# Two-layer hybrid decoder on one core: mixer operands without the norm's row factor, gates and branch products token-major

## The chip, the cores and the metric

The kernel runs on one core of a Trainium2 chip. Its time is the device time of one execution in microseconds (us), as the median of several runs. The engines are TensorE (PE, matmuls; PEld is its weight load), VectorE (DVE), ScalarE (ACT), GpSimd (POOL) and SyncE (SP, which issues most transfers). PE's results go to PSUM, which the kernel uses as eight banks; one bank holds a 128x512 tile of 32-bit numbers.

## What is computed

DEPTH = 2 layers over SEQ = 256 tokens with D_MODEL = 1024, all in 32-bit numbers:

```python
for l in range(DEPTH):
    h = rmsnorm(x, norm_mix[l])
    x = x + mixer_block(h, ...)
    x = x + cross_attention(rmsnorm(x, norm_xattn[l]), rmsnorm(mem, norm_mem[l]), ...)
    x = x + squared_relu_mlp(rmsnorm(x, norm_mlp[l]), w_up[l], w_down[l])
return rmsnorm(x, norm_final)

def rmsnorm(x, g):
    return x * rsqrt(mean(x * x, axis=-1, keepdims=True) + eps) * g

def mixer_block(h, ...):
    zin = h @ w_in
    (cq, ckv, kpe, sg_uv, gq, gk, gv, g_lr, g_og, dq, dk, dv, da, db, dz, gates) = split(zin)
    branches = stack([mla(...), spatial_gating(...), gla(...), deltanet(...)])  # 4 x (256, 256)
    proj = einsum('bsnw,nwd->bsnd', branches, w_branch)
    gate = sigmoid(gates).reshape(b, s, 4, 1024)
    return sum(gate * proj, axis=2) @ w_out
```

The factor `rsqrt(...)` of the norm is one number for each token (the row factor); `g` is one number for each of the 1024 features (the gain). A product of the normalised input can be taken without the row factor, and each row of the result multiplied by it.

## The kernel before

**Products.** A 32-bit operand is split into a high and a low part, and each product is three matmuls: high by high, low by high, high by low (`mm3`, L185 to L187). Weights arrive in order as a stream of blocks of 128x1024 (`half`): SP transfers two blocks at a time into one of three buffers, ACT casts the high part `wh` (L178), DVE subtracts for the low part `wl` (L181); four buffers each for `wh` and `wl` let this run ahead of PE. A buffer is written again only when PE has read it for the last time.

Two forms of product run on the stream. `gemm` keeps the weights as the stationary operand and moves 256 tokens past them, so its matmuls are 256 wide (N=256) and the result has features on the partitions. `gemm_tok` keeps 128 tokens as the stationary operand and moves 512 weight columns past them (N=512); its result is token-major: tokens on the partitions, one bank for each of two token halves t.

**Banks and pieces.** Three banks (tag "g") serve the streamed products, five (tag "s") all else. A bank is free when its eviction, an ACT or DVE instruction, has read it. Tiles of 128x512 in on-chip memory come from `new()`, a list of 44 pieces in which the piece freed first is given out first; `rel()` frees them. A new tile in a piece waits for the last reader of the old one.

**Order.** A scheduler decides before the run in what order each engine issues its instructions; on the chip each engine keeps that order, and waits on semaphores for the others. The gate products are independent of the mixers, so the order strews them between the mixers' small matmuls.

**A layer.** First `gemm` on `Norm.h`/`Norm.l`, which hold the input times the gain without the row factor; `ev_dn` multiplies by the row factor `rrow` when it evicts. Meanwhile the row factor is computed. Then `hn` = input × gain × row factor (L484, DVE), its high part `hh` (L487, ACT) and low part `hl` (L488, DVE). On these run `zin_rest` (four more column blocks and the token-major block `zs`), and the gates (L1077 evicts them through tanh, since sigmoid(z) = (tanh(z/2) + 1)/2). The mixers run beside the gates: among them the delta net (`dn_out`: L694 `u0`, L698, L703, L710, L724, where `uu` is evicted at L695 and L711) and the gated linear attention (`gla`: L789 makes the running sum `cum`, from it DVE makes the tiles `dd`, L814 to L821, ACT exponentiates them at L823, DVE multiplies them into `qt`, L856). `head_out` ends a branch; it makes a row factor `rb` (L774, ACT), turned by PE at L778.

Behind the mixers come the products on the memory (`mh`, `ml`; `mr` are its transfers, which ACT issues at L1110, `kx` the result), then `merge`: the four branch products of 128 features at a time, multiplied by the gates (L1092, DVE), added by POOL (L1093 and L1097), split into `mgh` and `mgl` (L1099, L1100), the operands of `w_out`. Cross attention and the MLP follow. The end of the program is a token-major product, whose eviction adds (L1239), squares (L1240, ACT), multiplies by the final gain `gf` (L1241, DVE) and scales (L1245, L1247).

Of the kernel before, what the change touches and what calls it, by code (L numbers as in the profile page):

```python
# [55 lines left out]
def decoder(ctx: ExitStack, tc: tile.TileContext, ws, xn_d, xt_d, mem_d, pos_d, fin_d, par_d, cst_d, msk_d, out_d):  # L56
# [59 lines left out]
    hh, hl = [], []  # L116
# [194 lines left out]
    class Norm:  # L311
        pass
# [33 lines left out]
    def gate_tile(i, dt=F32, name="gt"):  # L346
        return ap.tile([P, 2, T], dt, tag=f"gt{i}", name=nm(name))

    def operands(j, g, mix=False, parts=(slice(0, 2),), share=False):
        if mix and parts[0].start == 0:  # L350
            if j == 0:
                Norm.h, Norm.l = [], []
            Norm.h.append(gate_tile(2 * j, F32R, "xh")), Norm.l.append(gate_tile(2 * j + 1, F32R, "xl"))
        if True:
            dh, dl = (Norm.h[j], Norm.l[j]) if mix else (hh[j], hl[j])
            for p in parts:
                split_scaled(xs[j][:, p], g[:, 2 * j + p.start : 2 * j + p.stop], dh[:, p], dl[:, p], share)
# [67 lines left out]
    def layer(l):  # L425
# [50 lines left out]


        if l == 0:
            for d, n in ((hh, "hh"), (hl, "hl")):
                d.extend(ap.tile([P, 2, T], F32R, tag=f"{n}{j}", name=nm(n)) for j in range(4))  # L480
        for j in range(4):
            t = new(name="hn")
            for c in range(2):
# [4 lines left out]
            V.tensor_tensor(hl[j], t, hh[j].bitcast(F32), op=ALU.subtract)  # L488
# [594 lines left out]
        def merge(m):  # L1083
            wh, wl = half()
            for a in range(2):
                ps = pg.tile([P, 2, T], F32, tag="g", name=nm("g"))
# [5 lines left out]
                V.scalar_tensor_tensor(gt[m][a], gt[m][a], 1.0, ps, op0=ALU.add, op1=ALU.mult)  # L1092
            G.tensor_tensor(gt[m][0], gt[m][0], gt[m][1], op=ALU.add)  # L1093
# [344 lines left out]
```

## Time and profile before

| | |
|---|---|
| median of 3 runs | 1111.3 us (1110.27 to 1112.75) |
| profiled execution, its own time | 1111.81 us |
| its span in the trace | 1110.0 us |
| mean granted PE clock | 0.993 |
| PE busy | 1089.8 us, 8494 matmuls |
| DVE, ACT, POOL busy | 808.9, 586.8, 194.5 us |

The page of the profile lists the busy time of each engine, the chain that ended last (followed back from the last instruction to what released each step), and the costliest groups of instructions: line, engine, operation, tile written and tiles read, shapes, count, then busy time, mean duration in ns, and the idle time just before them with what ended it. Matmuls overlap, so a matmul's displayed duration is longer than the distance to the next one; the distance between starts is what PE spends. Rows of the timeline hold start, duration, engine, line, operation and tiles. The granted clock is the share of full speed that PE was given in a window.

### The profile page before, as it was taken

Reading aid. Unit: us, or ns where it says so; the run is one execution under the profiler, and the core shown is the slowest. Engines: PE = TensorE matmul, PEld = TensorE weight load, DVE = VectorE, ACT = ScalarE, POOL = GpSimd, SP = SyncE. Lnnn points to the kernel's source line nnn. Section 1 sums busy time; section 2 is a strip of 40 time slices with the busy share of each in tenths; the row PEclk is TensorE's granted clock in tenths of the full one; section 3 lists DMA queues with packets and bytes.
Section 4 is the critical chain, followed back from the end, with each engine's and each line's share of the span. In section 5 each row is a group of like instructions: output and inputs, shape, how many; then the busy total and the mean of one; then the engine's idle time right before and its main releaser. Section 6 shows DMA issues by size and latency. Waiting matters only on the chain.

```text
span 1110.0 us, 20715 instructions
## 1 busy us (share of the span) xinstructions
PE 1089.8 (98%) x8494; PEld 1046.4 (94%) x8494; DVE 808.9 (73%) x1411; ACT 586.8 (53%) x883; POOL 194.5 (18%) x176
## 2 busy tenths in 40 slices
PE   8899999999999999999999999999999999999996
PEld 8799999999998999999999899999999899998885
DVE  6999848779865866655679997686796777665454
ACT  6475564654644655544455646554454555555342
POOL 6223006108200200000102420310451011010000
PEclk9899999999999999999999999999999999999998
DMA  9344523454543455545545444244455334554541
GB/s 353 141 156 150 182 84 126 141 191 164 187 151 145 175 185 181 185 189 190 190 181 190 153 152 152 84 171 155 165 188 190 133 136 188 190 209 157 190 185 38
DMA packets 28319, 185.13 MB, mean 167 GB/s; under 512 B 3392, under 2 KB 3648, under 8 KB 6976
## 3 DMA queue, kind: packets, MB, share of 16 engines
q1 hardware_dynamic: 26208, 179.09, 44.3%
q10 hardware_dynamic: 2016, 4.72, 1.3%
q8 instruction: 66, 1.08, 0.4%
q14 instruction: 29, 0.24, 0.1%
HBM read 182.75 MB, written 1.05 MB: 166 GB/s over the span
## 4 chain that ended last, share of the span: by engine, by line
PE 94%; DVE 2%; DMA 1%; ACT 1%; issue 0%; ACTq 0%
PE g L186 28%; PE g L185 28%; PE g L187 28%; PE ps L185 1%; PE ps L186 1%; PE ps L187 1%; DMA mr<-memt 1%; PE ps L662 1%; PE ps L658 1%; PE ps L587 1%; DVE wl L181 1%; ACT wh L178 1%; DMA wr<-ws 0%; PE ps L575 0%; PE ps L967 0%
## 5 line engine op out<-in xcount | busy, mean ns | idle before, releaser
L181 DVE TENSOR_TENSOR wl<-wr,wh 128x1024 fp32r<-128x1024 f32 (+1 forms) x337 | 414.6, 1233 | 202.7 <-ACT wh L178 201.8
L178 ACT ACTIVATE wh<-wr 128x1024 fp32r<-128x1024 f32 (+1 forms) x337 | 355.0, 1057 | 352.1 <-PE g L186 254.4
L186 PE MATMUL g<-hl,wh 128*128 128x256 f32 x1280 | 362.5, 283 | 5.3 <-DVE hl L488 5.3
L187 PE MATMUL g<-hh,wl 128*128 128x256 f32 x1280 | 364.1, 285 | 0.0
L185 PE MATMUL g<-hh,wh 128*128 128x256 f32 x1280 | 362.8, 284 | 0.0
L186 PEld LDWEIGHTS g<-hl,wh 128*128 128x128 f32 x1280 | 242.3, 189 | 5.9 <-DVE hl L488 5.5
L187 PEld LDWEIGHTS g<-hh,wl 128*128 128x128 f32 x1280 | 242.0, 189 | 1.0 <-issue 0.3
L185 PEld LDWEIGHTS g<-hh,wh 128*128 128x128 f32 x1280 | 241.8, 189 | 0.7
L187 PE MATMUL g<-ah,wl 128*128 128x256 f32 x256 | 72.0, 281 | 0.0
L186 PE MATMUL g<-al,wh 128*128 128x256 f32 x256 | 71.9, 281 | 0.0
L185 PE MATMUL g<-ah,wh 128*128 128x256 f32 x256 | 71.8, 281 | 0.0
L325 POOL TENSOR_TENSOR sq<-sq,sq 128x512 f32<-128x512 f32 x14 | 21.1, 1506 | 244.8 <-ACT sq L317 244.6
L1093 POOL TENSOR_TENSOR gt<-gt,gt 128x512 f32<-128x512 f32 x16 | 35.6, 2227 | 92.8 <-DVE gt L1092 91.9
L186 PE MATMUL g<-wl,ah 128*128 128x512 f32 x128 | 50.2, 395 | 0.0
L187 PE MATMUL g<-wh,al 128*128 128x512 f32 x128 | 50.1, 394 | 0.0
L185 PE MATMUL g<-wh,ah 128*128 128x512 f32 x128 | 50.0, 395 | 0.0
L185 PEld LDWEIGHTS g<-ah,wh 128*128 128x128 f32 x256 | 48.2, 188 | 0.0
L187 PEld LDWEIGHTS g<-ah,wl 128*128 128x128 f32 x256 | 48.2, 188 | 0.0
L186 PEld LDWEIGHTS g<-al,wh 128*128 128x128 f32 x256 | 48.2, 188 | 0.0
L185 PE MATMUL g<-xh,wh 128*128 128x256 f32 x144 | 39.8, 282 | 1.5 <-ACT xh L298 1.5
L186 PE MATMUL g<-xl,wh 128*128 128x256 f32 x144 | 40.8, 285 | 0.3 <-DVE xl L307 0.3
L187 PE MATMUL g<-xh,wl 128*128 128x256 f32 x144 | 40.4, 283 | 0.0
(500 smaller groups left out, 2276.2 us busy)
## 6 DMA issues: line engine op xcount, KB each, us to landing
wr<-ws SPq DMA_DIRECT2D x166, 1024.0 KB, 4.8
wr<-ws ACTq DMA_DIRECT2D x4, 512.0 KB, 7.7
mr<-memt ACTq DMA_DIRECT2D x8, 256.0 KB, 4.0
par<-par SPq DMA_DIRECT2D x2, 778.0 KB, 6.9
x<-xt SPq DMA_DIRECT2D x3, 256.0 KB, 7.7
cst<-cst SPq DMA_DIRECT2D x1, 588.0 KB, 8.4
gf<-fin SPq DMA_DIRECT2D x2, 256.0 KB, 5.2
yt<-y ACTq DMA_DIRECT2D x2, 256.0 KB, 2.5
```

The lines of the kernel that those rows point to most:

```text
L178: i = S.activation(wh[:, p], r[:, p], AF.Copy)
L181: V.tensor_tensor(wl[:, p], r[:, p], wh[:, p].bitcast(F32), op=ALU.subtract)
L185: PE.matmul(out, ah, bh, start=start, stop=False)
L186: PE.matmul(out, ah, bl, start=False, stop=False)
L187: PE.matmul(out, al, bh, start=False, stop=stop)
L325: G.tensor_tensor(acc, acc, sq, op=ALU.add)
L587: PE.matmul(kk[o][:, 2 * i + c], kT[r, c, ts], src[r, c, ts], start=True, stop=True)
L658: PE.matmul(xp[:, h], M[:, h], Tm[:, h], start=True, stop=True)
L662: PE.matmul(up[:, h], X[t][:, h], U[:, h], start=True, stop=True)
L1093: G.tensor_tensor(gt[m][0], gt[m][0], gt[m][1], op=ALU.add)
```

## The change

The block that made `hn`, `hh` and `hl` for the mixer is removed. `zin_rest`, `zs` and the gates run on `Norm.h`/`Norm.l` (now X and XL) and the row factor enters where a result is evicted: as a row (`rrow`, DVE) for feature-major results, as a scale for each partition (`R.rs`, ACT) for token-major ones, halved (`R.rsh`) for the tanh. The gates become `gemm_tok`: 384 matmuls of N=512 in a layer instead of 768 of N=256. So do the branch products: 96 instead of 192. The merged product is then token-major; 16 PE transposes in a layer turn it, 8 for each half nb of the features, and ACT and DVE split it out of PSUM as 128x512. The additions run on POOL for n = 1 and 2 and on DVE for n = 3. The gate tiles of nb = 0 lie in the buffers of `hh`/`hl` (tags hx), those of nb = 1 in pieces. The host puts the weights in the new order. At the end of the program the last product with `gf` goes to a tile of its own.

```diff
     def operands(j, g, mix=False, parts=(slice(0, 2),), share=False):
...
+        dh, dl = (Norm.h, Norm.l) if mix else (hh, hl)
+        if parts[0].start == 0:
+            for i, d in enumerate((dh, dl)):
+                tag = f"xm{2 * j + i}" if mix else f"hx{2 * j + i}"
+                d[j] = ap.tile([P, 2, T], F32R, tag=tag, name=nm("xm" if mix else "hx"))
...
         def ev_dn(p, parts):
             if p == 0:
-                R.rrow = row_of(stat("rsmix"), name="rrow")
+                R.rs = stat("rsmix")
+                R.rrow = row_of(R.rs, name="rrow")
+                R.rsh = small(2, "rsh")
+                V.tensor_scalar(R.rsh, R.rs, 0.5, None, op0=ALU.mult)
...
-        for j in range(4):
-            t = new(name="hn")
-            for c in range(2):
-                V.scalar_tensor_tensor(
-                    t[:, c], xs[j][:, c], gain(4 * l)[:, 2 * j + c : 2 * j + c + 1], R.rrow, op0=ALU.mult, op1=ALU.mult
-                )
-            S.copy(hh[j], t)
-            V.tensor_tensor(hl[j], t, hh[j].bitcast(F32), op=ALU.subtract)
-            rel(t)
...
             def ev_rest(p, parts):
...
-                S.copy(t, ps)
+                V.tensor_tensor(t, ps, bc2(R.rrow), op=ALU.mult)
...
-            gemm(H, L, 8, 4, ev_rest)
+            gemm(X, XL, 8, 4, ev_rest)
...
-                S.copy(z, ps)
+                S.activation(z, ps, AF.Copy, scale=R.rs[:, t : t + 1])
...
-            gemm_tok(H, L, 8, ev_tok)
+            gemm_tok(X, XL, 8, ev_tok)
...
-        gt = [[None, None] for _ in range(8)]
-
-        def gates(m):
-            def evac(a, parts):
-                ps = parts[0][1]
-                if m < 4:
-                    t = gate_tile(2 * m + a)
+        gt = {}
+
+        def gates(nb, n):
+            def evac(t, ps):
+                if nb == 0:
+                    g = ap.tile([P, 512], F32, tag=f"hx{2 * n + t}", name=nm("gt"))
                 else:
-                    t = new(name="gt")
-                S.activation(t, ps, AF.Tanh, scale=0.5)
-                gt[m][a] = t
-            gemm(H, L, 8, 2, evac)
+                    g = new(shape=(P, 512), name="gt")
+                S.activation(g, ps, AF.Tanh, scale=R.rsh[:, t : t + 1])
+                gt[nb, n, t] = g
+
+            gemm_tok(X, XL, 8, evac)
 
         mgh, mgl = [], []
 
-        def merge(m):
-            wh, wl = half()
-            for a in range(2):
-                ps = pg.tile([P, 2, T], F32, tag="g", name=nm("g"))
-                for b in range(2):
-                    n = 2 * a + b
+        def merge(nb):
+            for n in range(4):
+                wh, wl = half()
+                for t in range(2):
+                    ps = pg.tile([P, 512], F32, tag="g", name=nm("g"))
+                    s = slice(128 * t, 128 * t + 128)
                     for k in range(2):
-                        c = slice(128 * (2 * n + k), 128 * (2 * n + k) + 128)
-                        mm3(ps[:, b], wh[:, c], wl[:, c], brh[n][:, k], brl[n][:, k], k == 0, k == 1)
-                V.scalar_tensor_tensor(gt[m][a], gt[m][a], 1.0, ps, op0=ALU.add, op1=ALU.mult)
-            G.tensor_tensor(gt[m][0], gt[m][0], gt[m][1], op=ALU.add)
-            if m % 2 == 0:
-                mgh.append(new(F32R, name="mgh")), mgl.append(new(F32R, name="mgl"))
-            t = gt[m][1][:, 0]
-            G.tensor_tensor(t, gt[m][0][:, 0], gt[m][0][:, 1], op=ALU.add)
-            dh, dl = mgh[-1][:, m % 2], mgl[-1][:, m % 2]
-            S.activation(dh, t, AF.Copy, scale=0.5)
-            V.scalar_tensor_tensor(dl, t, 0.5, dh.bitcast(F32), op0=ALU.mult, op1=ALU.subtract)
-            if m >= 4:
-                rel(gt[m])
-
-        for m in range(8):
-            gates(m)
+                        c = slice(512 * k, 512 * k + 512)
+                        mm3(ps, brh[n][:, k, s], brl[n][:, k, s], wh[:, c], wl[:, c], k == 0, k == 1)
+                    g, acc = gt[nb, n, t], gt[nb, 0, t]
+                    V.scalar_tensor_tensor(g, g, 1.0, ps, op0=ALU.add, op1=ALU.mult)
+                    if n:
+                        (V if n == 3 else G).tensor_tensor(acc, acc, g, op=ALU.add)
+            for j in range(2):
+                ps = bank()
+                for c in range(2):
+                    for t in range(2):
+                        o = 256 * j + 128 * c
+                        PE.transpose(ps[:, c, 128 * t : 128 * t + 128], gt[nb, 0, t][:, o : o + 128], ident)
+                a, b = new(F32R, name="mgh"), new(F32R, name="mgl")
+                S.activation(a, ps, AF.Copy, scale=0.5)
+                V.scalar_tensor_tensor(b, ps, 0.5, a.bitcast(F32), op0=ALU.mult, op1=ALU.subtract)
+                mgh.append(a), mgl.append(b)
+            if nb:
+                rel([gt[1, n, t] for n in range(4) for t in range(2)])
+
+        for nb in range(2):
+            for n in range(4):
+                gates(nb, n)
...
-        for m in range(8):
-            merge(m)
+        for nb in range(2):
+            merge(nb)
...
-                V.tensor_tensor(z, z, gf[nb], op=ALU.mult)
                 if nb == 0:
+                    V.tensor_tensor(z, z, gf[nb], op=ALU.mult)
                     return
+                u = yg[t]
+                V.tensor_tensor(u, z, gf[nb], op=ALU.mult)
...
-                V.tensor_scalar(y[t][1], y[t][1], rf, None, op0=ALU.mult)
-                S.dma_start(out_d[:, t, 512:1024], y[t][1])
+                V.tensor_scalar(u, u, rf, None, op0=ALU.mult)
+                S.dma_start(out_d[:, t, 512:1024], u)
```

The change also moves instructions, since the scheduler makes a new order. The rows below give line, operation, tile written, tiles read and size of a repetition; numbers behind a name tell buffers apart. Line numbers of the changed kernel are up to 16 lower (L774 is the old L789, L759 the old L774).

VectorE in layer 0, where the first product on the mixer operands behind `ev_dn` begins. Before (`cv` belongs to the short convolution, `gkv` and `y` are evictions):

```order
L535 SCALAR_TENSOR_TENSOR cv_572<-zc_294,par_105,cv_572 128x256
L181 TENSOR_TENSOR wl_701<-wr_698,wh_700 128x1024
L535 SCALAR_TENSOR_TENSOR cv_554<-zc_300,par_105,cv_554 128x256 x2
L466 TENSOR_TENSOR gkv_486<-g_427,rrow_292 128x512
L498 TENSOR_TENSOR y_521<-ps_518,par_105 128x272
L488 TENSOR_TENSOR hl_494<-hn_498,hh_490 128x512
L535 SCALAR_TENSOR_TENSOR cv_590<-zc_364,par_105,cv_590 128x256 x2
L181 TENSOR_TENSOR wl_729<-wr_698,wh_728 128x1024
L488 TENSOR_TENSOR hl_495<-hn_503,hh_491 128x512
L488 TENSOR_TENSOR hl_496<-hn_508,hh_492 128x512
L535 SCALAR_TENSOR_TENSOR cv_572<-zc_294,par_105,cv_572 128x256
L488 TENSOR_TENSOR hl_497<-hn_513,hh_493 128x512
```

After, around the same evictions of `gkv` and `y`:

```order
L467 TENSOR_TENSOR gkv_488<-g_429,rrow_292 128x512
L520 SCALAR_TENSOR_TENSOR cv_564<-zc_366,par_105,cv_564 128x256
L394 SCALAR_TENSOR_TENSOR a_595<-a_596,a_595 64x256
L520 SCALAR_TENSOR_TENSOR cv_546<-zc_296,par_105,cv_546 128x256
L181 TENSOR_TENSOR wl_703<-wr_672,wh_702 128x1024
L520 SCALAR_TENSOR_TENSOR cv_546<-zc_296,par_105,cv_546 128x256
L483 TENSOR_TENSOR y_495<-ps_492,par_105 128x272
L520 SCALAR_TENSOR_TENSOR cv_528<-zc_302,par_105,cv_528 128x256 x2
L520 SCALAR_TENSOR_TENSOR cv_564<-zc_366,par_105,cv_564 128x256
L181 TENSOR_TENSOR wl_736<-wr_733,wh_735 128x1024
L520 SCALAR_TENSOR_TENSOR cv_564<-zc_366,par_105,cv_564 128x256
L394 SCALAR_TENSOR_TENSOR a_595<-a_596,a_595 64x256
```

The four `hl` subtractions are gone from between the convolution's steps; evictions of `zin_rest` (`og`, L723) join the list further down, and the weight splits `wl` follow each other more closely.

TensorE in layer 0 around the product that makes `cum` (L789 before, L774 after). Before, with the gate product g_2303 going on in the gaps:

```order
L185 MATMUL g_2303<-hh_491,wh_2306 128x256
L186 MATMUL g_2303<-hl_495,wh_2306 128x256
L683 MATMUL ps_1459<-U_1283,X_1291 64x64 x4
L789 MATMUL ps_1465<-cst,la_550 128x128 x2
L694 MATMUL ps_1489<-bv_1094,U_1282 128x64 x4
L187 MATMUL g_2303<-hh_491,wl_2307 128x256
L185 MATMUL g_2303<-hh_492,wh_2306 128x256
L186 MATMUL g_2303<-hl_496,wh_2306 128x256
L187 MATMUL g_2303<-hh_492,wl_2307 128x256
```

After:

```order
L979 MATMUL ps_1410<-pt_1396,vt_1254 64x128
L664 MATMUL ps_1427<-T_1259,M_1023 64x64 x4
L668 MATMUL ps_1433<-U_1257,X_1265 64x64 x4
L774 MATMUL ps_1439<-cst,la_524 128x128 x2
L679 MATMUL ps_1463<-bv_1068,U_1256 128x64 x4
L683 MATMUL ps_1469<-uu_1462,kd_1061 128x128 x2
L688 MATMUL ps_1474<-s_256_1472,cv_528 128x128 x2
L185 MATMUL g_2099<-wh_2102,xm_117 128x512
L186 MATMUL g_2099<-wl_2103,xm_117 128x512
L187 MATMUL g_2099<-wh_2102,xm_118 128x512
L185 MATMUL g_2099<-wh_2102,xm_117 128x512
```

Before, the gate product g_2303 is in its first part when L789 comes, and its other 37 matmuls, the 48 of g_2364 and 28 of g_2425 lie between L694 and the delta net's L724. After, g_2098 has ended ahead of L668, and the next gate product, g_2099, stands behind L688 and first waits for a bank; between L774 and L709 (the old L724) there is only g_2099, 24 matmuls. Layer 1 has the same sequence from L774 on.

ScalarE a little later in layer 0, around `rb` of the delta net (L774 before, L759 after; `wh` are weight casts, `gt` gate evictions). Before:

```order
L1077 ACTIVATE gt_2423<-g_2364 128x512
L178 ACTIVATE wh_2611<-wr_2609 128x1024
L178 ACTIVATE wh_2639<-wr_2609 128x1024
L178 ACTIVATE wh_2672<-wr_2670 128x1024
L774 COPY rb_1628<-dny_1602 128x512
L178 ACTIVATE wh_2700<-wr_2670 128x1024
L1077 ACTIVATE gt_2545<-g_2486 128x512
```

After:

```order
L1061 ACTIVATE gt_2168<-g_2098,rsh_294 128x512
L178 ACTIVATE wh_2250<-wr_2248 128x1024
L178 ACTIVATE wh_2266<-wr_2248 128x1024
L178 ACTIVATE wh_2284<-wr_2282 128x1024
L178 ACTIVATE wh_2300<-wr_2282 128x1024
L759 COPY rb_1602<-dny_1576 128x512
L1061 ACTIVATE gt_2242<-g_2172,rsh_294 128x512
```

Before, three casts stand between the gate eviction and `rb`, after it is four. The fourth, wh_2300, takes the buffer of wh_2226, which the gate product g_2173 reads until its last matmul, and on PE L763 (the turn of `rb`) stands right behind that matmul.

More of the change, by code (lines that the diff above doesn't have):

```diff
@@ L115, in decoder @@
     xs += [cp.tile([P, 2, T], F32, name=f"x{j}") for j in range(1, 4)]
-    hh, hl = [], []
+    hh, hl = [None] * 4, [None] * 4
     cs = cp.tile([P, T], F32, name="cs")
@@ L311, in decoder @@
     class Norm:
-        pass
+        h, l = [None] * 4, [None] * 4
     def squares(j, src, parts=(slice(0, 2),), hold=False):
@@ L344, in gain @@
         return nrm[:, 8 * i : 8 * i + 8]
-    def gate_tile(i, dt=F32, name="gt"):
-        return ap.tile([P, 2, T], dt, tag=f"gt{i}", name=nm(name))
     def operands(j, g, mix=False, parts=(slice(0, 2),), share=False):
[L350 to L357, printed above, removed]
+        dh, dl = (Norm.h, Norm.l) if mix else (hh, hl)
[3 more added lines that the diff above has]
+                d[j] = ap.tile([P, 2, T], F32R, tag=tag, name=nm("xm" if mix else "hx"))
+        for p in parts:
+            split_scaled(xs[j][:, p], g[:, 2 * j + p.start : 2 * j + p.stop], dh[j][:, p], dl[j][:, p], share)
     def residual(g, mix=False, row=None):
@@ L442, in layer @@
         H, L = ch(hh), ch(hl)
+        X, XL = ch(Norm.h), ch(Norm.l)
         zc = []
@@ L475, in layer @@
             later(cst[:, C_TRI:C_N], cst_d[:, C_TRI:C_N])
-        if l == 0:
-            for d, n in ((hh, "hh"), (hl, "hl")):
-                d.extend(ap.tile([P, 2, T], F32R, tag=f"{n}{j}", name=nm(n)) for j in range(4))
-        for j in range(4):
-            t = new(name="hn")
-            for c in range(2):
-                V.scalar_tensor_tensor(
-                    t[:, c], xs[j][:, c], gain(4 * l)[:, 2 * j + c : 2 * j + c + 1], R.rrow, op0=ALU.mult, op1=ALU.mult
-                )
-            S.copy(hh[j], t)
-            V.tensor_tensor(hl[j], t, hh[j].bitcast(F32), op=ALU.subtract)
-            rel(t)
         def soft_gates():
@@ L1233, in final @@
         sq = new(shape=(P, 512), name="sq")
+        yg = [new(shape=(P, 512), name="yg") for _ in range(2)]
         for nb in range(2):
@@ L1319, in _stream @@
         h.append(u)
-        for m in range(8):
+        for nb in range(2):
             for n in range(4):
-                h.append(_half_a(cols(GATES + 1024 * n + 128 * m)))
+                h += tok(cols(GATES + 1024 * n + 512 * nb, 512))
         wb = np.asarray(i["w_branch"][l])
         h += _proj(i["xattn_wk"][l])
-        for m in range(8):
-            b = wb[:, :, 128 * m : 128 * m + 128].reshape(4, 2, P, P)
-            h.append(b.transpose(2, 0, 1, 3).reshape(P, 1024))
+        for nb in range(2):
+            for n in range(4):
+                h += tok(wb[n][:, 512 * nb : 512 * nb + 512])
         h += _proj(i["w_out"][l]) + _proj(i["xattn_wq"][l])
```

4 lines of the change are left out of this document (1 added, 3 removed).

## The prediction

> **What bounds the kernel now.** I read the page first, then the waits of TensorE (PE), then windows around the one long wait, then the timeline of the stage in which the change reorders most.
>
> ```profile
> span 1110.0 us, 20715 instructions
> ...
> PE 1089.8 (98%) x8494; PEld 1046.4 (94%) x8494; DVE 808.9 (73%) x1411; ACT 586.8 (53%) x883; POOL 194.5 (18%) x176
> ...
> PE 94%; DVE 2%; DMA 1%; ACT 1%; issue 0%; ACTq 0%
> ```
>
> PE is busy 98% of the span and is 94% of the chain that ended last. So only two things count: how long PE's own instructions are, and whether PE is made to wait. Work that leaves or joins VectorE (DVE) or ScalarE (ACT) is worth nothing by itself.
>
> The waits of PE (line, who ended it: total, times, longest) name the two that the change can touch:
>
> ```profile
> PE g L186 <- DVE hl L488: 5.3, 1, 5.3
> ...
> PE ps L880 <- DVE sc L873: 1.3, 2, 0.8
> ```
>
> The first happens once, in layer 0: the first product on the normalised operands waits for `hl`. Windows around it (length, busy PE, PEld, DVE, ACT, POOL, granted clock):
>
> ```profile
> 34.00:39.00 5.00, 5.00 (x45) 4.87 (x43) 5.00 (x12) 4.01 (x9) 0.00 (x0) 1.00 0.00 0
> 39.00:44.50 5.50, 0.47 (x3) 0.26 (x2) 5.44 (x11) 2.62 (x5) 0.25 (x1) 0.83 0.53 192
> 44.50:50.00 5.50, 5.25 (x26) 5.22 (x27) 5.44 (x11) 0.00 (x0) 0.90 (x1) 0.54 0.38 131
> ```
> ```profile
> 45.12 0.42 PE L187 MATMUL g<-hh,wl 128*128 128x256 f32 x1
> ...
> 45.98 0.41 PE L185 MATMUL g<-hh,wh 128*128 128x256 f32 x1
> ```
>
> DVE is full in all three. The wait is followed by 5.5 us at a granted clock of 0.54, so it costs more than its 5.3 us.
>
> **What the change removes.** The `hn`/`hh`/`hl` block goes; the products behind it read operands that exist already. (1) The wait: −5.3. (2) The clock behind it: PE works there at about half rate: the two timeline rows are four starts apart, 0.86/4 = 0.215 us each, where 0.119 is usual (next rows). The 26 matmuls of the window lose up to 26 × 0.096 = 2.5; the first and last are partly outside it, I take −2.2. DVE takes over four evictions of 0.68 us from ACT in each layer (the kind of L466), but gives up eight multiplies and four subtractions there, so it has less to do.
>
> ```profile
> 149.78 0.28 PE L186 MATMUL g<-hl,wh 128*128 128x256 f32 x1
> ...
> 152.04 0.29 PE L187 MATMUL g<-hh,wl 128*128 128x256 f32 x1
> ...
> 1079.76 0.39 PE L186 MATMUL g<-wl,ah 128*128 128x512 f32 x1
> ...
> 1084.84 0.39 PE L187 MATMUL g<-wh,al 128*128 128x512 f32 x1
> ```
>
> (3) Wider matmuls. The first two rows are 19 starts apart: 2.26/19 = 0.1189 us for N=256. The last two are 22 apart: 5.08/22 = 0.2309 for N=512. One wide matmul replaces two narrow ones and saves 0.0069 us. There are 768 − 384 pairs in the gates and 192 − 96 in the merge of each layer: 384 + 96 = 480, in two layers 960, so −6.6. The bounds are 0 (no gain) and this. The Trainium skill (TensorE: Matmul & The Clock Gate, section Back-to-back issue gap) gives an isolated gap of N/2.4 ns plus 2.5 ns, by which a pair would save only 2.5 ns and the sum below would be 1119.6; the rows are further apart than its gaps at both sizes, so I go by the rows.
>
> **What it adds.**
>
> ```profile
> 1009.65 1.75 PE ps L1230 x16
> ...
> 1101.43 0.73 ACT sq L1240 x2
> 1102.18 0.69 DVE y L1241
> ```
>
> (4) 16 transposes of 128x128 a layer: sixteen of the same kind took 1.75 us at L1230, so two layers +3.5. (5) The first eight of a layer stand between two pieces of the merge and have their input early. The last eight stand ahead of `w_out`; of that product, 36 narrow matmuls on the first half of `mgh` stand ahead of them, 36 × 0.119 = 4.3 us, and cover the last DVE addition and the POOL addition ahead of it (2.2 us each, row L1093 below). What remains is the ACT copy and the DVE split behind the transposes, 0.59 + 0.68 by the rows of L1231 and L488, less 0.3 of transposes and 0.3 of matmuls that still run: between 0 and 1.3, I take 1.0 a layer, +2.0. (6) At the end the multiply by `gf` no longer waits for the square, which now runs beside it: the chain held 0.69 for it, −0.7.
>
> ```profile
> L1093 POOL TENSOR_TENSOR gt<-gt,gt 128x512 f32<-128x512 f32 x16 | 35.6, 2227 | 92.8 <-DVE gt L1092 91.9
> ...
> L1231 ACT COPY y<-ps 128x512 f32<-128x512 f32 x4 | 2.1, 587 | 0.0
> ...
> L488 DVE TENSOR_TENSOR hl<-hn,hh 128x512 fp32r<-128x512 f32 x8 | 5.2, 679 | 0.0
> ```
>
> **What it moves: the fill of the mixers.** The gate products are PE's filling while the mixers' chains run on the other engines. The order shows that L789 (now L774, the product that makes `cum`) stood before with the gate products only partly used; now all that the three banks allow stand ahead of it, in both layers. What follows L789 in the trace of before:
>
> ```profile
> 167.22 0.71 PE L789 MATMUL ps<-cst,la 128*128 128x128 f32 x4
> ...
> 186.03 0.43 PE L724 MATMUL ps<-dec,uu 128*64 128x128 f32 x2
> ```
> ```profile
> L187 PE MATMUL g<-hh,wl 128*128 128x256 f32 x38 | 10.9, 287 | 0.0
> L185 PE MATMUL g<-hh,wh 128*128 128x256 f32 x38 | 10.7, 282 | 0.0
> L186 PE MATMUL g<-hl,wh 128*128 128x256 f32 x37 | 10.6, 287 | 0.0
> ```
> ```profile
> 168.37 0.29 DVE L820 TENSOR_TENSOR dd<-cum 128x128 f32<-128x128 f32 x1 [0.75 <-ACT cum L791]
> ...
> 172.18 0.62 DVE L815 TENSOR_SCALAR dd<-cum 128x128 f32<-128x128 f32 x1
> 172.38 1.21 DVE L181 TENSOR_TENSOR wl<-wr,wh 128x1024 fp32r<-128x1024 f32 x1
> 173.51 1.30 DVE L856 TENSOR_TENSOR qt<-dd,qbd 128x128 f32<-128x128 f32 x4
> ...
> 184.14 0.41 DVE L711 TENSOR_TENSOR uu<-ps,bro 128x256 f32<-128x256 f32 x1
> ```
>
> From the end of L789 at 167.93 to the start of L724 at 186.03 PE had 18.1 us of work without a gap: 113 gate matmuls (the three rows of the lines in that window: 38 + 38 + 37), 113 × 0.1189 = 13.4, and 4.7 us of mixer matmuls. L724 needs `uu`, which DVE finished at 184.55, so 16.6 us after L789, busy nearly throughout. PE was the later of the two by 1.5 us. (7) In the changed order there are 24 wide gate matmuls between the same two lines: 24 × 0.2309 = 5.5, with the 4.7 makes 10.2 us. The DVE list between them is the same but for one of four weight splits (1.13 from 172.38 to 173.51): 16.6 − 1.1 = 15.5. PE waits 15.5 − 10.2 = 5.3 us. It waits in pieces: for `uu` at L683, for `s1` at L688, then for the gate bank, whose eviction (0.58) takes a piece that the `dd` instructions free at 172.80, last at L709. Lower bound: the bank alone, 172.80 − 167.93 + 0.58 = 5.5, less 1.7 of L679, L683 and L688, is 3.8. Upper: all four splits stay, 6.4. I take 5.3 in each of two layers, +10.6. Queued behind it on PE are the rest of the gates, so nothing overtakes.
>
> ```profile
> 742.23 1.06 ACT L178 ACTIVATE wh<-wr 128x1024 fp32r<-128x1024 f32 x1 [1.78 <-PE g L186]
> 744.14 0.62 ACT L774 COPY rb<-dny 128x512 f32<-128x512 f32 x1 [0.84 <-DVE dny L771]
> ```
>
> (8) The rows of ACT show `rb` (now L759) behind a weight cast. In the new order that cast reuses a buffer which the 24 matmuls just ahead of L763 read to the last, and L763 waits for `rb`. So PE ends its matmuls, then waits 1.06 + 0.62 + about 0.1 = 1.8. Bounds 0 (the cast's buffer free earlier) and 1.9; I take 1.8 a layer, +3.6. (9) These delays give DVE time, so that L880's 1.3 us should go: −1.3.
>
> **The sum**, against the profiled execution at 1111.8 (span 1110.0; the median of three is 1111.3, so 0.5 lower): 1111.8 − 5.3 − 2.2 − 6.6 + 3.5 + 2.0 − 0.7 + 10.6 + 3.6 − 1.3 = **1115.4**. The gains (−16.1) are real but smaller than what the shortened fill takes (+14.2) with the transposes and the waits behind them (+5.5).
>
> **Rivals.** (A) The fill suffices. PE comes to L774 late enough that DVE's list is short, or the `uu` chain is not bound by the splits in between; then (7) and (8) fall away and the time is 1101.2, faster. For it speaks that DVE is busy 73% only. Against it: `dd` needs `cum`, which PE itself makes at L774, so DVE cannot start before, and the rows show it busy from 168.37 on. It decides if DVE needs under 10.2 us from L774 to `uu`. Chance 0.20. (B) Only the bank holds PE, 3.8 a layer, and `rb` is in time: 1115.4 − 3.0 − 3.6 = 1108.8. Chance 0.15. (C) The new idle time halves the clock as the old one did. The windows show 0.54 behind 5.3 us of idle time; 2.2 us in each layer makes 1119.8. Against it: the new idle time is cut by matmuls into pieces of about 1.3, 2.8 and 1.2 us, and behind the waits of L880 no such loss is seen. The Trainium skill (the same page, section Part 1: The HAM clock gate) says that the array falls to half rate after an idle window of about 3.4 us, which agrees with the old wait and would spare the pieces. Chance 0.12. (D) The wide matmuls bring nothing, so that the change doesn't do on PE what it says: without (3) the time is 1122.0. It would come about if two banks in turn, with mixer matmuls between them, cost what the width saves. Against it: the 22 starts at 0.2309 are of the same form, weights moving over fixed activations. Chance 0.06. The forecast keeps 0.47.
>
> **Range and chances.** The likeliest is 1115.4, its own range 1111 to 1118 by the bounds of (5), (7) and (8). With B and C and part of A and D, 8 in 10 lie in 1105 to 1121. What a measurement here can tell from no change is about 0.2%, 2.2 us: below 1109.1 is faster (A and half of B, 0.27), above 1113.5 slower (C, D and most of the forecast, 0.57), between them 0.16.
>
> **What would show it.** PE's waits should lose L488, and the clock stay at 1.0 around 39 to 50 us. PE should show waits at L683, L688, at a gate matmul, at L709 and at L763, together some 7 us a layer. Gate matmuls should start 0.231 us apart. If PE's waits behind L774 are under 2 us a layer, (7) is wrong and A holds; if the clock drops there, C; if the merges are not shorter, D.

## The result, and the profile after

| | before | after |
|---|---|---|
| median | 1110.6 us (1110.27 to 1112.75, 5 runs) | 1122.8 us (1122.27 to 1123.0, 5 runs) |
| ratio | | 1.0105, 95% interval 1.009 to 1.012 |
| profiled execution, its span | 1111.81, 1110.0 us | 1122.87, 1121.1 us |
| mean granted clock | 0.993 | 0.988 |

The change makes the kernel 1% slower. The sign was forecast, but the time lies 7 us above the forecast and outside the range. The page of after, its span, PE's busy time and the engines of its chain:

```profile
span 1121.1 us, 18769 instructions
...
PE 1090.5 (97%) x7566; PEld 995.1 (89%) x7566; DVE 805.1 (72%) x1397; ACT 582.9 (52%) x859; POOL 172.3 (15%) x160
...
PE 89%; DVE 7%; ACT 2%; issue 1%; POOL 0%; DMA 0%; ACTq 0%
```

PE has 928 matmuls fewer and is busy as long as before. In the chain that ended last DVE went from 2% to 7%. PE's waits in after (total, times, longest) say where:

```profile
PE ps L688 <- DVE s L685: 4.2, 2, 2.1
PE ps L763 <- ACT rb L759: 3.5, 2, 1.7
PE g L186 <- DVE wl L181: 3.2, 3, 2.1
PE ps L683 <- DVE uu L680: 2.6, 2, 1.3
...
PE g L185 <- ACT wh L178: 1.0, 1, 1.0
...
PE g L185 <- ACT mgh L1088: 0.7, 2, 0.4
...
PE ps L1086 <- DVE gt L1080: 0.6, 2, 0.3
...
PE g L185 <- DVE gt L1078: 0.4, 2, 0.2
```

The waits for `hl` and at L880 are gone. New are L683 and L688 (`uu`, `s`), L763 (`rb`), which the prediction named, and waits for the weight parts `wl` and `wh`, which it did not. The wait at L709, which it named too, is not there. The last three rows are the merge's. Windows of after, where the old wait was, then around 95 us, then behind L774 (length, busy PE, PEld, DVE, ACT, POOL, clock):

```profile
39.00:44.50 5.50, 5.50 (x50) 5.50 (x49) 5.44 (x12) 2.02 (x2) 0.00 (x0) 1.00 0.39 162
...
90.00:95.00 5.00, 3.88 (x20) 2.63 (x18) 4.77 (x14) 3.32 (x8) 2.33 (x2) 1.00 0.13 52
95.00:100.00 5.00, 2.93 (x7) 2.10 (x8) 4.93 (x9) 1.42 (x2) 1.31 (x2) 0.78 0.00 0
100.00:105.00 5.00, 5.00 (x39) 4.14 (x38) 3.07 (x9) 1.30 (x2) 0.00 (x0) 0.88 0.59 210
...
170.00:175.00 5.00, 4.49 (x55) 3.63 (x54) 0.69 (x1) 1.54 (x4) 0.00 (x0) 1.00 0.29 123
175.00:180.00 5.00, 1.93 (x16) 1.60 (x14) 4.18 (x18) 1.14 (x3) 3.19 (x2) 0.97 0.00 0
180.00:185.00 5.00, 4.68 (x13) 3.91 (x14) 4.87 (x16) 2.70 (x4) 5.00 (x7) 0.50 0.00 0
185.00:190.00 5.00, 5.00 (x24) 4.12 (x24) 5.00 (x9) 2.84 (x4) 3.67 (x6) 0.85 0.01 3
```

At 39 us PE now works through at full clock. But DVE is as full there as before, and at 92 to 98 us PE idles and then runs at a reduced clock. Behind L774 DVE does 0.69 us of work in the 5 us ahead of `cum`, then is full, PE waits, and the clock falls to 0.50; by the windows it stays there for some 6.8 us.

The time by stages, from the first matmul of one product to the first of the next, the last to the end of its last matmul (us, worked out from the traces; the columns e5 to e10 are experiments below):

| stage | before | after | e5 token-major alone | e6 operands alone | e7 | e8 | e10 |
|---|---|---|---|---|---|---|---|
| layer 0, mixers and gates | 216.4 | 219.3 | 218.5 | 216.9 | 212.7 | 218.6 | 215.4 |
| memory product, merge, `w_out` | 69.8 | 74.1 | 73.9 | 70.0 | 70.0 | 70.0 | 70.0 |
| cross attention and MLP | 265.2 | 264.4 | 265.3 | 264.3 | 264.4 | 263.9 | 264.3 |
| layer 1, mixers and gates | 206.5 | 212.4 | 214.1 | 210.6 | 210.2 | 204.6 | 207.6 |
| memory product, merge, `w_out` | 69.5 | 73.5 | 73.6 | 69.5 | 69.5 | 70.1 | 69.4 |
| cross attention and MLP | 265.5 | 261.0 | 265.3 | 261.0 | 261.0 | 260.4 | 261.0 |

After loses 2.8 and 5.9 us in the mixers, 4.2 and 4.0 from the memory product to `w_out`, and gains 0.9 and 4.6 in stages that the change doesn't touch.

The first row compares only in part. The traces of before, after, e1, e2, e7, e8 and e10 hold 3.4 us at half clock near 9 us, those of the other runs none; here are after and e4, an experiment below:

```profile
8.00:13.00 5.00, 4.70 (x26) 4.50 (x26) 4.69 (x8) 4.73 (x9) 4.26 (x3) 0.66 1.05 427
```
```profile
8.00:13.00 5.00, 4.70 (x40) 4.50 (x39) 4.58 (x8) 4.63 (x9) 4.15 (x3) 1.00 1.05 425
```

The first 48 matmuls of the first product take 13.4 to 13.5 us in before and after and 11.9 to 12.0 without it, so the layer 0 mixers of e5 and e6 count 1.5 us more beside before or after. This doesn't go with the kernel: e11 has the instructions of after and e12 those of before, and neither trace holds it.

### The profile page after: what moved, and what is told of

It reads as the page before. It is cut to its first block, busy times and chain, and to the rows that moved or that the text cites. A ratio compares the mean times of both kernels' runs of the same rounds, so it can differ in the third digit from the quotient of the medians.

```text
span 1121.1 us, 18769 instructions
## 1 busy us (share of the span) xinstructions
PE 1090.5 (97%) x7566; PEld 995.1 (89%) x7566; DVE 805.1 (72%) x1397; ACT 582.9 (52%) x859; POOL 172.3 (15%) x160
## 4 chain that ended last, share of the span: by engine, by line
PE 89%; DVE 7%; ACT 2%; issue 1%; POOL 0%; DMA 0%; ACTq 0%
PE g L186 26%; PE g L187 26%; PE g L185 26%; DVE wl L181 3%; DVE gt L1078 1%; PE ps L846 1%; PE ps L186 1%; PE ps L187 1%; PE ps L185 1%; ACT wh L178 1%; PE ps L643 1%; PE ps L647 1%; DMA wr<-ws 0%; PE ps L952 0%; DVE mgl L1089 0%
## 5 line engine op out<-in xcount | busy, mean ns | idle before, releaser
L187 PE MATMUL g<-hx,wl 128*128 128x256 f32 x640 | 178.3, 279 | 0.0
L186 PE MATMUL g<-hx,wh 128*128 128x256 f32 x640 | 178.3, 279 | 0.0
L185 PE MATMUL g<-hx,wh 128*128 128x256 f32 x640 | 178.2, 279 | 0.0
L186 PE MATMUL g<-wl,xm 128*128 128x512 f32 x288 | 117.7, 409 | 3.2 <-DVE wl L181 3.2
L185 PEld LDWEIGHTS g<-hx,wh 128*128 128x128 f32 x640 | 120.8, 189 | 0.0
L186 PEld LDWEIGHTS g<-hx,wh 128*128 128x128 f32 x640 | 120.7, 189 | 0.0
L187 PEld LDWEIGHTS g<-hx,wl 128*128 128x128 f32 x640 | 120.1, 188 | 0.0
L185 PE MATMUL g<-wh,xm 128*128 128x512 f32 x288 | 116.7, 413 | 1.9 <-ACT wh L178 1.0
L187 PE MATMUL g<-wh,xm 128*128 128x512 f32 x288 | 117.5, 409 | 0.0
L185 PE MATMUL g<-xm,wh 128*128 128x256 f32 x272 | 75.4, 281 | 1.5 <-ACT xm L298 1.5
L186 PE MATMUL g<-xm,wh 128*128 128x256 f32 x272 | 76.4, 282 | 0.3 <-DVE xm L307 0.3
L187 PE MATMUL g<-xm,wl 128*128 128x256 f32 x272 | 76.2, 282 | 0.0
L186 PEld LDWEIGHTS g<-wl,xm 128*128 128x128 f32 x288 | 55.7, 194 | 16.6 <-DVE wl L181 4.4
L185 PEld LDWEIGHTS g<-wh,xm 128*128 128x128 f32 x288 | 55.8, 194 | 16.0 <-ACT gt L1061 1.6
L187 PEld LDWEIGHTS g<-wh,xm 128*128 128x128 f32 x288 | 55.8, 194 | 12.8 <-issue 0.3
```

What stands on the lines that cost most here:

```text
L185: PE.matmul(out, ah, bh, start=start, stop=False)
L186: PE.matmul(out, ah, bl, start=False, stop=False)
L187: PE.matmul(out, al, bh, start=False, stop=stop)
```

## The experiments

Before took 1110.5 to 1111.7 us beside them; each ratio is to before on the same chip. Theory 1: what costs in the mixers is the place of `cum` in PE's order. Theory 2: DVE is full at the start of layer 0, and the removed wait is paid there again. Theory W came later: the token-major gates take the filling away from between the delta net's products; its rival O puts that on the operands.

**e1, `cum` early.** The matmul and the copy that make `cum` go ahead of the attention branch.

```diff
@@ gla
-            cump = bank((P, T))
...
-            S.copy(cum, cump)
+            cum = R.cum
@@ others
             yield from gmlp()
+            cump = bank((P, T))
...
+            S.copy(R.cum, cump)
             yield from mla()
```

> The changed kernel with the product that makes cum, and its copy, moved ahead of the latent attention, so that DVE can make dd while PE still has gate products. Theory 1 (the gate products are used up ahead of cum, and PE then waits for DVE): the waits at L683 and L688 (6.8 us) and the slow clock behind them go, and the time falls from 1122.8 by 9 to 13 us. Rival (the mixers as a whole are bound by DVE, whatever stands first): the waits only move, under 3 us are gained.

Measured 1123.8 us, ratio 1.0121 (1.0106 to 1.0136). PE's waits shrink (L683 1.6, L688 1.0) and a new one comes for `r` (2.1), but layer 1's mixers take 212.5 us, as in after; layer 0's take 217.4, 1.9 less. Windows of e1 in layer 1:

```profile
730.00:735.00 5.00, 2.85 (x14) 2.39 (x14) 4.29 (x17) 0.00 (x0) 0.00 (x0) 0.71 0.64 210
735.00:740.00 5.00, 5.00 (x31) 4.22 (x32) 2.29 (x10) 1.23 (x3) 1.74 (x3) 0.50 0.17 54
740.00:745.00 5.00, 5.00 (x25) 3.92 (x23) 0.90 (x4) 2.13 (x5) 1.02 (x2) 0.76 0.15 52
```

Now DVE has time (0.90 us of 5) and PE is the one that is late, because it works at half clock behind the shortened waits: `uu` of L696 is ready 2.7 us ahead of L709. So Theory 1 falls as stated: the place of `cum` alone gives nothing in layer 1. The whole also holds 3.2 us of another kind: layer 1's up-projection is nearly as slow here as in before.

**e2, `rb` on DVE.**

```diff
-            S.copy(rb, rn.unsqueeze(2).to_broadcast([P, 8, 64]))
+            V.tensor_copy(rb, rn.unsqueeze(2).to_broadcast([P, 8, 64]))
```

> The changed kernel with the copy that makes rb on DVE instead of ACT. Theory 1b (rb stands on ACT behind a weight cast that waits for the last gate matmul): the two waits at L763 (3.5 us) fall to under 0.5 each, the time by about 3. Rival (rb waits for the chain of small DVE steps, which ends at the same moment): under 1 us is gained, and the wait names DVE.

Measured 1127.5 us, ratio 1.015 (1.0133 to 1.0166): slower by 4.8 than after. L763 then waits 5.7 us for DVE instead of 3.5 for ACT. DVE is the engine that is late there, so nothing may be added to it.

**e3, the waits filled.** Three dummy matmuls ahead of L683's and five ahead of L688's, written over by the real ones.

```diff
+            for _ in range(3):
+                PE.matmul(flat(s1p), kd[:, 0:128], bv[:, 0], start=True, stop=True)
...
+            for _ in range(5):
+                PE.matmul(flat(ksp), kd[:, 0:128], flat(uu[:, 0:4]), start=True, stop=True)
```

> The changed kernel with 3 matmuls that count for nothing ahead of the wait at L683 and 5 ahead of the one at L688 in each layer (their results are written over), so that PE is not idle there. Both theories: the granted clock stays near 1.0 in the 7 us behind. Theory C1 (the slow clock costs what it slows): the time falls by about 4.5 us. Theory C2 (the DVE chain to uu ends just ahead of L709 anyway): PE waits at L709 instead, and the time falls by 0 to 1.5 us.

Measured 1128.1 us, ratio 1.016 (1.0145 to 1.0175): slower by 5.4 than after. Waits and a window of e3:

```profile
PE ps L767 <- ACT rb L763: 4.9, 2, 3.1
PE ps L713 <- DVE uu L700: 3.6, 2, 1.8
```
```profile
185.00:190.00 5.00, 4.50 (x33) 3.62 (x31) 5.00 (x7) 3.71 (x7) 5.00 (x7) 1.00 0.24 64
190.00:195.00 5.00, 3.53 (x20) 2.92 (x21) 5.00 (x16) 1.27 (x3) 0.68 (x1) 0.60 0.50 169
```

The clock is saved up to 190 us and nothing is won: the same wait stands behind the gate matmuls, at L713 (the old L709), where `uu` isn't ready, and the clock falls there instead. DVE's list behind `cum` sets this stretch; in after the half clock lies beside it. The loss of 5.4 us neither theory foresaw: the mixers are 3.3 and 3.7 us longer than in after, and what of this the eight matmuls cost themselves isn't separated.

**e4, three evictions on POOL.** `og`, `dz` and `su` by an ACT copy and a POOL multiply.

```diff
-                V.tensor_tensor(t, ps, bc2(R.rrow), op=ALU.mult)
+                if p == 2:
+                    V.tensor_tensor(t, ps, bc2(R.rrow), op=ALU.mult)
+                else:
+                    S.copy(t, ps)
+                    G.tensor_tensor(t, t, bc2(R.rrow), op=ALU.mult)
```

> The changed kernel with three of the four evictions of the second projection (og, dz, su) copied by ACT and multiplied by POOL, which takes 2 us of work from DVE ahead of 95 us. Theory 2 (PE's wait of 3.9 us at 93 to 97 us in layer 0 is DVE being full since the start, so the old stall is paid there): that wait falls to about 2 us, and the time by 2 to 4 us. Rival (that wait is a matter of the order in which DVE does the weight splits): it stays within 0.7 us of what it was.

Measured 1118.4 us, ratio 1.0074 (1.0059 to 1.0089). Windows of e4:

```profile
90.00:95.00 5.00, 4.47 (x21) 3.39 (x20) 4.93 (x19) 2.70 (x4) 0.00 (x0) 1.00 0.45 143
95.00:100.00 5.00, 5.00 (x23) 3.95 (x21) 4.75 (x14) 2.10 (x4) 2.09 (x2) 1.00 0.61 215
```

With three evictions less on DVE, PE lacks 0.5 us of 10 between 90 and 100 us (3.2 in after), and the clock stays at 1.0. But a wait of 2.0 us for `wl` has come up earlier:

```profile
75.49 0.50 PE L186 MATMUL g<-wl,xm 128*128 128x512 f32 x1 [1.96 <-DVE wl L181]
```

Layer 0's mixers take 214.9 us, 4.4 less than in after, of which 1.5 is the half clock near 9 us that this trace lacks; some 2.9 us are left, within the 2 to 4 expected. Layer 1's take 212.3, as in after. So work taken off DVE helps, as Theory 2 says, but part of the wait only moved. The rival named beforehand, the order of the weight splits, is not ruled out: DVE makes one at 85.3 us in after and the next at 95.4, in e4 the same gap lies between 79.8 and 90.4, and all orders were made anew.

**e5, the token-major part alone.** Before, with the gates, branch products, transposes and weight order of after, on `hh` and `hl`:

```diff
@@ before.py: gates, merge
-            gemm(H, L, 8, 2, evac)
+            gemm_tok(H, L, 8, evac)
```

> Before with one part of the change: gates and branch products token-major, transposes behind the merge; the normalised operands hn, hh, hl stay, also for zin_rest, and so do the plain evictions. In layer 1 the mixers (first projection to first memory product) took 206.5 us before and 212.4 after. Theory W (the token-major gates take the filling away from between the delta net's products; in the new order nothing stands between L694, L698 and L703, as in after): 211 to 213 us in layer 1, waits at L698 and L703 of 1.3 and 2 us in each layer, the wait for hl of 5.3 stays; in all 1120 to 1129. Rival O (the operands without the row factor, with their evictions on VectorE, do it): layer 1 stays at 204 to 207 us, no such waits; in all 1110 to 1115.

**e6, the operands alone.** After, with the feature-major gates and merge of before:

```diff
@@ after.py: gates, merge
-            gemm_tok(X, XL, 8, evac)
+            gemm(X, XL, 8, 2, evac)
...
-                S.activation(g, ps, AF.Tanh, scale=R.rsh[:, t : t + 1])
+                V.tensor_tensor(t, ps, bc2(R.rrow), op=ALU.mult)
+                S.activation(t, t, AF.Tanh, scale=0.5)
```

> After with feature-major gates and merge as before: the operands without the row factor alone, with the row factor applied by VectorE at the gates' eviction ahead of the tanh (16 more multiplies of 128x512 in a layer) and with the end of the program as in after. Theory W: gate matmuls stand between the delta net's products again, mixers of layer 1 204 to 208 us, no wait over 1 us at L683 or L688 there; the start of layer 0 still pays for the full VectorE near 93 us; in all 1106 to 1113. Rival O: mixers of layer 1 211 to 213 us, in all 1116 to 1122. A third outcome: the 16 multiplies (0.58 us each, 9.3 us a layer) lengthen VectorE's chain and new waits for gate banks show, 1113 to 1118.

Measured: e5 1129.2 us, ratio 1.0163 (1.0146 to 1.018); e6 1110.5 us, ratio 1.0001 (0.9991 to 1.001). PE's waits, first of e5 (its L698 and L703 are L683 and L688 of after), then of e6:

```profile
PE ps L778 <- ACT rb L774: 4.9, 2, 3.1
PE ps L703 <- DVE s L700: 3.7, 2, 2.1
PE ps L698 <- DVE uu L695: 2.6, 2, 1.3
```
```profile
PE g L185 <- DVE gt L1062: 6.5, 5, 2.0
...
PE ps L688 <- DVE s L685: 1.9, 1, 1.9
PE ps L763 <- ACT rb L759: 1.8, 2, 1.5
```

For e5 Theory W holds, and more strongly than expected: with the old operands the token-major part brings the waits for `uu`, `s` and `rb` as after has them, and the 4 us from the memory product to `w_out` in each layer; the wait for `hl` stays (5.5 us). Without it the waits at L683 are gone, and L688 and L763 halve. In e6 16 multiplies a layer on DVE hold the gate banks instead (the first row), so layer 1's mixers still take 4.1 us longer than before (210.6, where W said 204 to 208). The whole time is W's, the waits are those of the third outcome.

**e7 and e10, the operands with DVE relieved.** e7 is e6 with the edit of e4. e10 also evicts the gates by an ACT copy and multiplies them on POOL:

```diff
@@ e10, gates
-                V.tensor_tensor(t, ps, bc2(R.rrow), op=ALU.mult)
+                S.copy(t, ps)
+                G.tensor_tensor(t, t, bc2(R.rrow), op=ALU.mult)
                 S.activation(t, t, AF.Tanh, scale=0.5)
```

> The run before, with three of the four zin_rest evictions in each layer as a ScalarE copy and a POOL multiply. Theory 2 (VectorE is full in the start of layer 0), by the 4.4 us that the same edit gave to the changed kernel: 3 to 5 us below the run of the operands alone, all of it in the mixers of layer 0. If it is within 1 us of that run, VectorE's load at the start is not what the stage waits for in this order.

> The operands without the row factor, three zin_rest evictions on POOL (the seventh run), and the feature-major gates evicted by a ScalarE copy, multiplied by POOL, and then sent through the tanh: no VectorE work in a gate's eviction. If the gate-bank waits of that run (6.6 us in all) came from VectorE's multiplies, they go and the whole is 1097 to 1102; if they came from VectorE's other load or if ScalarE, with 16 more copies of 0.6 us a layer, takes its place, 1103 to 1107.

Measured: e7 1105.5 us, ratio 0.9953 (0.9939 to 0.9968), 4.9 below e6, in layer 0's mixers, as said. But the start of that stage is not all of it: from 175 to 182.5 us, behind a wait of 1.9 us at L688, e6 has a mean clock of 0.54, and e7, without that wait, 1.00. e10 1106.1 us, ratio 0.9953 (0.9937 to 0.997): the gate-bank waits fall from 6.6 to 0.5 us and layer 1 gains 2.7, but waits for `wl` rise from 2.9 to 7.2 and layer 0 loses 2.7. The wait moved once more.

**e8, only `zin_rest` and `zs` on the new operands.** Before, with those evicted as in e4; `hn`, `hh` and `hl` are made behind `zin_rest`, for the gates.

```diff
-            gemm(H, L, 8, 4, ev_rest)
+            gemm(X, XL, 8, 4, ev_rest)
...
-            gemm_tok(H, L, 8, ev_tok)
+            gemm_tok(X, XL, 8, ev_tok)
```

> Before with the smallest part of the change: only zin_rest and zs run on the operands without the row factor (og, dz, su evicted by ScalarE and multiplied by POOL, cq by VectorE, zs by ScalarE with the factor as a scale); hn, hh and hl are made later, for the gates alone, which stay feature-major. By theory W the waits behind cum stay as before (none over 1 us at L685 or L690); by theory 2 the wait for hl and the clock behind it go without a new wait near 93 us: mixers of layer 0 208 to 211 us (216.5 before, 219.3 after), layer 1 205 to 208 us, in all 1102 to 1106. If the late hn block comes to stand in VectorE's way, 1107 to 1112.

Measured 1105.4 us, ratio 0.9951 (0.9936 to 0.9966). The whole is as expected, but by luck: layer 0's mixers take 218.6 us, longer than before's, where 208 to 211 was expected. PE waits 5.9 us for `wl` and 3.8 for gate banks in this kernel, most of it there: the `hn` block has come to stand in DVE's way. The gain is in layer 1's mixers (1.9 us) and in the last stage (5.1), whose code is the same.

**e9, the filling held back.** After, with an order edge on PE alone: a gate product's two halves (nb = 1, n = 1) start behind the delta net's u0.

```diff
@@ dn_out
+            Norm.mark = i.ins.name
@@ mm3
+        if start and Norm.hold is not None:
+            tc.add_manual_dep(i.ins, Norm.hold, ...
@@ gates
+            Norm.hold = Norm.mark if (nb, n) in ((1, 1),) else None
```

In its order 24 gate matmuls stand between u0 and L683's product and 22 between that and L688's, where after has none.

> After with one gate product (nb = 1, n = 1, two times 24 wide matmuls) held back in PE's order: its first matmul comes behind the delta net's u0 (L679), so that 24 matmuls stand between u0 and L683's product and 22 between that and L688's; nothing else of the instructions changes. Theory W (the filling was used up ahead of cum): the waits for uu and s (6.8 us in all in after) and the half clock behind them go, the product that makes cum starts 4 to 6 us earlier, the mixers of layer 1 take 206 to 209 us (212.4 in after), the whole 1112 to 1117. Rival S (the held matmuls were needed where they stood: the triangular solve ahead of cum now waits as long as the delta net did): mixers of layer 1 211 to 214 us, waits of PE in the solve (L672, L676) of 2 us or more a layer, the whole 1120 to 1126.

Measured 1118.5 us, ratio 1.0074 (1.0044 to 1.0103), with an unusual spread: five executions took 1115.5, 1116.5, 1118.5, 1123.3 and 1123.5 us, at mean clocks of 0.997, 0.995, 0.994, 0.989 and 0.989. The profiled one is one of the last two; its waits and windows (its L676, L704 and L772 are L668, L695 and L763 of after):

```profile
PE ps L704 <- DVE r L700: 3.7, 2, 1.9
PE ps L772 <- ACT rb L768: 3.5, 2, 1.7
PE ps L676 <- ACT X L673: 3.5, 4, 1.5
```
```profile
185.00:190.00 5.00, 5.00 (x29) 4.22 (x29) 3.98 (x15) 1.02 (x3) 1.11 (x2) 0.50 0.85 315
190.00:195.00 5.00, 5.00 (x24) 4.00 (x21) 0.90 (x4) 1.42 (x4) 1.64 (x2) 0.50 0.19 61
```

The waits for `uu` and `s` are gone, as W says; about as much waiting stands in the solve and for `r`, as S says. Neither wins: moving 48 matmuls moves the waits. Behind them the clock falls, and here DVE has time (0.90 us of 5), so the half clock counts: the five times of this one program spread over 8 us, in step with their mean clocks.

**e11 and e12, other buffers.** After and before, with the list of pieces turned by three places ahead of layer 1's up-projection; each engine's order is the same.

```diff
-        ah, al = [], []
+        ah, al = [rel(new(name="skip")) for _ in range(3 if l else 0)] and [], []
```

> After with the list of pieces turned by three places ahead of layer 1's up-projection: every engine has the same instructions in the same order, only the buffers of the MLP's intermediate tiles differ. The up-projection's matmuls of layer 1 stand 0.1133 us apart in after and 0.1187 in before. If the places of these tiles set that, the distance changes to 0.1165 or more and the time rises by 2 to 4 us; if not, it stays within 0.0005 of 0.1133 and the time within 1 us of 1122.8.

> The same turn of the list in before. If the places of the intermediate tiles set the distance of the up-projection's matmuls, it may leave 0.1187 here (0.1133 would make the whole 1106.5); if not, it stays and the time is within 1 us of 1110.6.

Measured 1120.7 and 1110.4 us (one run each); the matmuls there stay 0.1133 and 0.1187 us apart. The places of these tiles don't set the distance. e11 is 2.1 us below after, more than the 1 us expected; its trace lacks the half clock near 9 us, which is 1.5 of it.

## Why the prediction was wrong

By stages, its terms say for layer 0's mixers −7.5 (1, 2) − 2.65 (3) + 5.3 (7) + 1.8 (8) − 0.65 (9) = −3.7, and 2.8 was measured; for layer 1's +3.8, and 5.9; from the memory product to `w_out` 2 × (1.75 + 1.0 − 0.66) = +4.2, and 8.2; for the rest nothing, and −5.4; at the end −0.7, as measured. With 0.2 at the start the differences add to 7.5, the whole error.

**(1) and (2), the failing step.** The wait and its clock went as forecast. The step failed at its last sentence, that DVE "gives up eight multiplies and four subtractions there, so it has less to do". The windows quoted in the prediction had DVE full in all three. What left its list was replaced at once by what waited behind: from 33 to 93 us of after it is busy 57.1 of 60 us. PE ran on at 39 us and met the full engine later, where two weight splits stand 10 us apart. PE in after, near 95 us, and DVE just ahead of its last wait:

```profile
92.94 0.40 PE L187 MATMUL g<-wh,xm 128*128 128x512 f32 x1
94.38 1.08 PE L185 MATMUL g<-wh,xm 128*128 128x512 f32 x2 [1.04 <-ACT wh L178]
97.53 0.62 PE L186 MATMUL g<-wl,xm 128*128 128x512 f32 x1 [2.07 <-DVE wl L181]
97.95 0.63 PE L187 MATMUL g<-wh,xm 128*128 128x512 f32 x1
```
```profile
95.04 0.41 DVE L593 TENSOR_TENSOR kd<-ps,ekd 128x256 f32<-128x256 f32 x1
95.38 2.09 DVE L181 TENSOR_TENSOR wl<-wr,wh 128x1024 fp32r<-128x1024 f32 x1
```

From 92.94 to 97.53 three matmuls start (the second row holds two), 0.7 us at 0.233 each, so 3.9 us are lost; the next two stand 0.42 apart, and 3.4 us at this half clock lose another 1.7. So (1) and (2) are worth some −2 (−7.5, plus 3.9, plus 1.7), not −7.5. Less work on DVE wins back some 2.9 us of this (e4); whether the rest hangs on its load or on the order of its splits stays open.

**(3), width: mis-sized.** Of the gates of after, 18 starts apart:

```profile
202.12 0.40 PE L187 MATMUL g<-wh,xm 128*128 128x512 f32 x1
...
206.32 0.40 PE L187 MATMUL g<-wh,xm 128*128 128x512 f32 x1
```

4.20/18 = 0.2333 us, not 0.2309: a pair saves 0.0045 and not 0.0069, 0.9 us a layer less in the gates. The prediction took the distance from another product. In the merge of each layer the width brought nothing: 23.3 us before, 23.5 after without its eight transposes, since short waits and slow matmuls stand at its weight blocks.

**(7), right in what sets it, too small.** L774 ends at 175.4 and L709 starts at 192.0 in layer 0, 16.6 us for 10.2 of own work: 6.4 and not 5.3, in layer 1 6.2. The second `uu` (L696) is ready 16.1 us behind L774, where 15.5 was forecast, and L709 starts 0.6 and 0.4 us later. But PE's loss has other pieces: 3.4 us of waits at L683 and L688, none at the gate bank or at L709, and 24 gate matmuls that take 8.3 us instead of 5.6, half of them at half clock. DVE in layer 1 of after, where the same happens:

```profile
722.78 0.69 DVE L437 TENSOR_TENSOR brl<-ps,brh 128x512 fp32r<-128x512 f32 x1 [5.65 <-ACT brh L436]
...
727.00 0.42 DVE L680 TENSOR_TENSOR uu<-ps,bro 128x256 f32<-128x256 f32 x1
...
729.78 0.42 DVE L685 TENSOR_TENSOR s<-ps,cst 128x256 f32<-128x256 f32 x1
730.11 3.39 DVE L841 TENSOR_TENSOR qt<-dd,qbd 128x128 f32<-128x128 f32 x8
733.42 0.41 DVE L690 TENSOR_TENSOR r<-ps,eg 128x256 f32<-128x256 f32 x1
...
740.99 0.41 DVE L696 TENSOR_TENSOR uu<-ps,bro 128x256 f32<-128x256 f32 x1
```

DVE idles 5.65 us while PE works off gates, then `uu`, `s` and `r` stand in one queue with the `dd` and `qt` of the linear attention. e5 and e6 show that the token-major part brings this, e3 that DVE's list and not the clock sets it in after, e9 that the missing filling makes the waits where they stand. Why the order made before the run spends the token-major gates earlier is not settled.

**Rival C** stood at 0.12, with the argument that the pieces would spare the clock. They did not: 0.50 at 180 to 185 us, behind waits of 1.3 and 2.1. In after it costs little, because DVE's chain is as long (e3); in e1 and e9 it counts, where L709 (L718 in e9) starts 1.3 to 2.7 us behind `uu`. The idle window of about 3.4 us that the Trainium skill gives (TensorE: Matmul & The Clock Gate, section Part 1: The HAM clock gate) was read as sparing the pieces, and the trace disagrees with that reading: PE was busy 1.93 of 5 us without one idle time of 3.4. The same page of the Trainium skill tells, in its section A second HAM failure mode: psum-queue depth-cycling, of a kernel in which frequent short idle times between groups of matmuls make the clock swing, and the windows here (1.93 of 5 us busy, then 0.50) look like that.

**(8), (4) and (6)** were right: L763 waits 1.7 us a layer, the first eight transposes of a layer take 0.8 us, and the end is 0.7 us shorter. **(9)** was right: L880's wait is gone. **(5)** named the waits rightly (the merge's three rows add to 1.7 us), yet from the memory product to `w_out` 4.0 us more were lost than forecast. By the starts in the traces 1.7 of them lie in the two memory products, 1.6 of it sixteen small matmuls (L743) that stood ahead of them in before (L758); 1.5 in the merges, most of it the width that brought nothing; 0.8 in `w_out`. e5 loses as much in this stage as after and e6 next to nothing, so it belongs to the token-major part.

**An unforecast gain** of 4.1 us lies in layer 1's up-projection, whose code is the same. Two rows of before, then of after, 27 starts apart each:

```profile
959.77 0.28 PE L186 MATMUL g<-hl,wh 128*128 128x256 f32 x1
...
962.97 0.28 PE L186 MATMUL g<-hl,wh 128*128 128x256 f32 x1
```
```profile
959.73 0.28 PE L186 MATMUL g<-hx,wh 128*128 128x256 f32 x1
...
962.79 0.28 PE L186 MATMUL g<-hx,wh 128*128 128x256 f32 x1
```

3.20/27 = 0.1185 and 3.06/27 = 0.1133 us. The product lasts 93.3 us in before and e5, 92.4 in e1, and 89.2 in after, e2 to e4 and e6 to e10. Without this gain after would be 1.5% slower; of the 0.5% that e7, e8 and e10 gain, most is this, and no run shows what makes it.

## What to carry to other kernels

Where an engine is full for a long stretch (here 57 of 60 us), a wait that is taken away ahead of it can come back behind it: ask which instruction stands next in its queue, and who waits for that. Independent work that covers a chain is worth something only beside the chain, so compare how much of it is left when the chain begins, not only its total length. Wider matmuls that cost fillings, transposes and more waits can lose several times what they save: here under 2 us a layer, for a loss on balance of 8 us in layer 0 and 11 in layer 1 (e5, with the 1.5 us of the clock near 9 us).

## What the runs showed of the hardware

- Matmuls of N=256 of one product stood 0.1133 us apart in some programs and 0.1178 to 0.1187 in others, at a granted clock of 1.0 and steadily over 90 us. The operand (e8 has that of before, at 0.1133), its buffers (e1 and after use the same, at 0.1178 and 0.1133) and the places of the results' tiles (e11, e12) don't explain it. The cause is open.
- Waits of 1.3 and 2.1 us with four small matmuls between them were followed by a clock of 0.50 for 6.8 us in both layers of after; behind the same waits in layer 0 of e5 it fell for only 3.4 us (0.66 over 180 to 185 us).
- The same instructions ran with 3.4 us at half clock near 9 us and without (after and e11, before and e12); it cost 1.5 us.
- In e9 one program took 1115.5 to 1123.5 us, in step with the mean clock, 0.997 to 0.989.
